# A four-layer hybrid block on one core: the weight sum of the third Strassen product made by GpSimd in SBUF instead of by an adding transfer

## The chip, the core and the metric

The kernel runs on one core of a Trainium2 chip. The metric is the device time of one execution in microseconds, median of three: 2467.82 us (2465.43 to 2470.07).

## The reference, cut to what matters

Four layers, each a mixer (RWKV-7, sliding-window attention, a spatial gating unit, gated linear attention) followed by a SwiGLU feed-forward part. Everything is float32, 512 tokens by 1024 features, 2816 hidden columns.

```python
def swiglu(x, w_in, w_out):
    gate, up = jnp.split(x @ w_in, 2, axis=-1)
    return (jax.nn.silu(gate) * up) @ w_out
...
    for i in range(DEPTH):
        hn = rmsnorm(h, norm_mix[i])
        ...
        h = h + m
        h = h + swiglu(rmsnorm(h, norm_ffn[i]), ffn_w_in[i], ffn_w_out[i])
    return rmsnorm(h, norm_final)
```

## The kernel before, in words

**The products.** Large matrix products go through `seven` (L857). It cuts the product into a 2 by 2 grid of halves and does it in seven half-size products instead of eight, with sums of weight quarters and of input quarters on the way. In the order of the code these are m1 (with weight quarter 0), m2 (quarter 1), m5 (quarters 2+0), m3 (quarter 3), m6 (2+0+3), m7 (3+2) and m4 (2+0+3+1). `load(q)` fetches a quarter into raw buffers `wraw`, issued by SP; `add(tile, q)` adds a quarter to a raw buffer that is already filled, by a transfer issued by GpSimd that accumulates while it lands. In the code `a`, `e`, `b`, `c` are the buffers of quarters 0, 1, 2, 3. So `a` and `e` are used once, `c` is added to once, and `b` three times: +0, +3, +1.

**Two pieces.** A quarter is held in two buffers ("first and second piece") of 128 partitions by 1024, 768 or 512 floats. Each piece is fetched, added to and split by itself.

**The split.** TensorE runs one-pass float32r products. So `mm` (L882) splits each raw buffer into a high part `whi` (a copy by ScalarE) and a low part `wlo` (raw minus high, by VectorE; `split`, L604) and does three matmuls for each tile. A product of width 512 is 24 matmuls of 128x512.

**Buffers.** The raw pool `wr` has 8 buffers: four quarters. `whi` and `wlo` have 4 buffers each: two quarters. PSUM has 8 banks.

**Where `seven` is called.** In each feed-forward layer (`ffn`, L809) there are six calls for the hidden columns (`hidden`, L933, weights `ffn_w_b` of width 384 and `ffn_w_a` of width 512) and three for the way back (`out_fast`, L838, weights `ffn_o_b` and `ffn_o_a`). The first two products of the next hidden block (its `a` and `e`) are done ahead of a way-back call, the other five behind it. The gating unit calls it four times, the linear attention three times in this form and twice with `rows=True`. That makes 43 calls that the change touches, with two pieces each.

**What sets the order.** No engine's order is written by hand. `Program` records every operation, then `run` (L309) places them one at a time: for each engine the ready operation with the lowest turn (its place in the code, moved by the table TURNS), if a buffer for it can be had, on a clock kept from the estimated costs in `price` (L283). A GpSimd addition is priced by `2.4` ns an element there, a transfer by 1000 ns of its engine and a shared DMA time. So an operation with another engine and cost moves others around it. On the chip each engine runs its list in order and waits by semaphores; a GpSimd transfer whose buffer isn't ready holds up all that is behind it on GpSimd, and an SP load that has no free buffer holds up all loads behind it.

All operations are recorded by one helper, so most rows of the profile have the line L253; the names of the tiles tell them apart.

Of the kernel before, what the change touches and what calls it, by code (L numbers as in the profile page):

```python
# [501 lines left out]
class K:  # L502
# [354 lines left out]
    def seven(self, w, W, x, nsub=4, rows=False):  # L857

        nc = self.nc
        m = 1024 // W
        us = [(k, min(m, nsub - k)) for k in range(0, nsub, m)] if rows else [(k, min(2, nsub - k)) for k in range(0, nsub, 2)]

        def load(q):  # L870
            t = []
            for k, n in us:
                raw = self.wr.tile([P, 1024], F32, name="wraw")[:, :n * W]
                nc.sync.dma_start(raw, w[q][:, k * W:(k + n) * W])
                t.append(raw)
            return t

        def add(a, q):
            for (k, n), t in zip(us, a):
                nc.gpsimd.dma_start(t, w[q][:, k * W:(k + n) * W], accum_op=ALU.add)  # L880

        def mm(key, ps, raw, first, last):  # L882
            xs = x(key)
            for u, (k0, n) in enumerate(us):
                hi = self.wh.tile([P, 1024], F32R, name="whi")[:, :n * W]
                lo = self.wl.tile([P, 1024], F32R, name="wlo")[:, :n * W]
                self.split(raw[u], hi, lo)
                if rows:
                    for j in range(W // P):
                        for k in range(n):  # L890
                            xh, xl = xs[(k0 + k) // 2]
                            t = slice((k0 + k) % 2 * 256, (k0 + k) % 2 * 256 + 256)
                            c = slice(k * W + j * P, k * W + (j + 1) * P)
                            self.mm3(ps[:, j * 256:(j + 1) * 256], hi[:, c], lo[:, c], xh[:, t], xl[:, t],
                                     first and k0 + k + j == 0, last and k0 + k == nsub - 1)
                    continue
                for b in range(2):
                    for k in range(n):
                        if callable(xs):
                            (xh, xl), t = xs(k0 + k), slice(b * P, (b + 1) * P)  # L900
                        else:
                            (xh, xl), t = xs[u], slice(k * 256 + b * P, k * 256 + (b + 1) * P)
                        c = slice(k * W, (k + 1) * W)
                        self.mm3(ps[b], xh[:, t], xl[:, t], hi[:, c], lo[:, c], first and k0 + k == 0, last and k0 + k == nsub - 1)
        banks = lambda: self.bank() if rows else [self.bank()[:, :W] for _ in range(2)]
        a = load(0)
        p = banks()
        mm('x11', p, a, True, True)
        yield 'm1', p
        e = load(1)  # L910
        s = banks()
        mm('x12', s, e, True, True)
        yield 'm2', s
        b = load(2)
        add(b, 0)
        r = banks()
        mm('s5', r, b, True, True)
        yield 'm5', r
        c = load(3)
        add(b, 3)  # L920
        t = banks()
        mm('s3', t, c, True, True)
        yield 'm3', t
        add(c, 2)
        mm('s6', p, b, False, True)
        yield 'm6', p
        mm('s7', p, c, False, True)
        yield 'm7', p
        add(b, 1)
        mm('x22', p, b, False, True)  # L930
        yield 'm4', p
# [1115 lines left out]
```

## Time and profile before

| | |
|---|---|
| median of three runs | 2467.82 us |
| the profiled execution, whole | 2470.02 us |
| its span on the core | 2468.3 us |
| mean granted clock | 0.997 |
| ScalarE busy | 1389.3 us (56%) |
| VectorE busy | 1930.5 us (78%) |
| GpSimd busy | 400.2 us (16%), 456 instructions |
| loads by SP (queue q1) | 226.47 MB, 27.2% of the 16 DMA engines |
| adding transfers by GpSimd (queue q0) | 171.99 MB, 39.2% of the 16 DMA engines |

The profiled execution's own time stands 1.7 us above its span, and 2.2 us above the median of the runs. Sums in the prediction are made against that execution. TensorE's two rows are matmuls (PE) and weight loads (PEld), which overlap.

### The profile page before, as it was taken

Reading aid. Unit: us, or ns where it says so; the run is one execution under the profiler, and the core shown is the slowest. Engines: PE = TensorE matmul, PEld = TensorE weight load, DVE = VectorE, ACT = ScalarE, POOL = GpSimd, SP = SyncE. Lnnn points to the kernel's source line nnn. Section 1 sums busy time; section 2 is a strip of 40 time slices with the busy share of each in tenths; the row PEclk is TensorE's granted clock in tenths of the full one; section 3 lists DMA queues with packets and bytes.
Section 4 is the critical chain, followed back from the end, with each engine's and each line's share of the span. In section 5 each row is a group of like instructions: output and inputs, shape, how many; then the busy total and the mean of one; then the engine's idle time right before and its main releaser. Section 6 shows DMA issues by size and latency. Waiting matters only on the chain.

```text
span 2468.3 us, 37524 instructions
## 1 busy us (share of the span) xinstructions
PE 2411.1 (98%) x14166; PEld 1995.9 (81%) x14166; DVE 1930.5 (78%) x3051; ACT 1389.3 (56%) x2267; POOL 400.2 (16%) x456
## 2 busy tenths in 40 slices
PE   9999999999999999999999999999999999999998
PEld 7677789987888768988887788887878788888886
DVE  8686995786779885777789886976868978886868
ACT  4545544664646476656466544854546756755555
POOL 0000000111112241121111300211111221212111
PEclk9999999999999999999999999999999999999999
DMA  5220002589898234898988835889897775989885
GB/s 170 71 71 10 11 11 81 137 226 215 208 221 187 75 107 103 192 238 192 233 189 202 218 99 153 183 201 216 200 225 182 187 181 124 187 214 227 216 211 125
DMA packets 128629, 400.85 MB, mean 162 GB/s; under 512 B 14384, under 2 KB 21040, under 8 KB 128448
## 3 DMA queue, kind: packets, MB, share of 16 engines
q0 software_dynamic: 50688, 171.99, 39.2%
q1 hardware_dynamic: 77760, 226.47, 27.2%
q8 instruction: 111, 1.82, 0.3%
q14 instruction: 70, 0.57, 0.1%
HBM read 393.95 MB, written 2.10 MB: 160 GB/s over the span
## 4 chain that ended last, share of the span: by engine, by line
PE 71%; DMA 9%; DVE 9%; ACT 5%; issue 4%; POOL 1%; SPq 0%; DVEq 0%; POOLq 0%; ACTq 0%
PE ps L253 71%; DMA wraw<-ffn_w_a 3%; DMA wraw<-ffn_w_b 2%; DVE wlo L253 2%; ACT slot L253 2%; DVE slot L253 2%; DMA wraw<-ffn_o_a 2%; ACT whi L253 1%; DVE h L253 1%; POOL wraw L253 1%; DVE et L253 1%; DMA wraw<-sg_w_v 1%; DVE mt L253 0%; DMA wraw<-gla_w_qk 0%; POOL slot L253 0%
## 5 line engine op out<-in xcount | busy, mean ns | idle before, releaser
L253 PE MATMUL ps<-whi,slot 128*128 128x512 f32 (+1 forms) x4960 | 1509.7, 385 | 13.7 <-DVE slot L253 7.4
L253 PEld LDWEIGHTS ps<-whi,slot 128*128 128x128 f32 x4960 | 923.4, 188 | 186.2 <-DVE slot L253 14.7
L253 ACT CAST whi<-wraw 128x1024 fp32r<-128x1024 f32 (+2 forms) x680 | 673.8, 997 | 619.5 <-PE ps L253 426.6
L253 DVE TENSOR_TENSOR wlo<-wraw,whi 128x1024 fp32r<-128x1024 f32 (+2 forms) x680 | 783.7, 1161 | 237.9 <-ACT whi L253 233.8
L253 PE MATMUL ps<-wlo,slot 128*128 128x512 f32 (+1 forms) x2480 | 932.7, 383 | 4.1 <-DVE wlo L253 4.1
L253 PEld LDWEIGHTS ps<-wlo,slot 128*128 128x128 f32 x2480 | 466.8, 188 | 85.7 <-DVE wlo L253 7.9
L253 PE MATMUL ps<-slot,whi 128*128 128x512 f32 (+3 forms) x976 | 276.1, 366 | 1.8 <-ACT slot L253 0.9
L253 DVE TENSOR_TENSOR slot<-ps,slot 128x512 f32<-128x512 f32 (+2 forms) x269 | 159.0, 607 | 79.7 <-PE ps L253 70.6
L253 PEld LDWEIGHTS ps<-slot,whi 128*128 128x128 f32 (+2 forms) x976 | 170.4, 184 | 40.4 <-issue 4.5
L253 POOL DMA_DIRECT2D wraw<-ffn_w_a x128 | 111.0, 879 | 483.2 <-DVE wlo L253 339.4
L253 DVE TENSOR_TENSOR h<-h,ps 128x512 f32<-128x512 f32 x240 | 159.0, 684 | 26.6 <-PE ps L253 24.3
L253 DVE TENSOR_TENSOR slot<-left,slot 128x512 fp32r<-128x512 f32 x250 | 160.2, 662 | 23.5 <-ACT slot L253 15.4
L253 PE MATMUL ps<-slot,wlo 128*128 128x512 f32 (+3 forms) x488 | 176.5, 366 | 0.0
L253 ACT CAST slot<-left 128x512 fp32r<-128x512 f32 (+1 forms) x250 | 143.4, 601 | 29.0 <-PE ps L253 18.0
L253 ACT COPY slot<-ps 128x512 f32<-128x512 f32 (+2 forms) x154 | 85.3, 566 | 72.4 <-PE ps L253 66.0
L253 PEld LDWEIGHTS ps<-slot,wlo 128*128 128x128 f32 (+2 forms) x488 | 89.5, 184 | 18.4 <-issue 3.7
L253 POOL DMA_DIRECT2D wraw<-ffn_o_a x64 | 55.9, 873 | 297.3 <-DVE wlo L253 210.5
L253 POOL DMA_DIRECT2D wraw<-ffn_w_b x64 | 55.1, 867 | 300.2 <-DVE wlo L253 99.4
L253 PE MATMUL ps<-ident,slot 128*128 128x128 f32 (+2 forms) x672 | 88.8, 265 | 6.6 <-DVE slot L253 6.4
L253 PEld LDWEIGHTS ps<-ident,slot 128*128 128x128 f32 (+2 forms) x672 | 68.8, 140 | 31.1 <-DVE slot L253 10.6
L253 DVE TENSOR_TENSOR slot<-slot 128x512 fp32r<-128x512 f32 (+7 forms) x131 | 77.2, 611 | 12.1 <-DMA slot<-slot 7.2
L253 ACT COPY left<-ps 128x512 f32<-128x512 f32 x100 | 51.0, 555 | 44.1 <-PE ps L253 44.0
(281 smaller groups left out, 2242.0 us busy)
## 6 DMA issues: line engine op xcount, KB each, us to landing
wraw<-ffn_w_a SPq DMA_DIRECT2D x128, 512.0 KB, 6.4
wraw<-ffn_w_a POOLq DMA_DIRECT2D x128, 512.0 KB, 7.9
wraw<-ffn_o_a SPq DMA_DIRECT2D x64, 512.0 KB, 5.1
wraw<-ffn_o_a POOLq DMA_DIRECT2D x64, 512.0 KB, 7.1
wraw<-ffn_w_b SPq DMA_DIRECT2D x64, 384.0 KB, 4.0
wraw<-ffn_w_b POOLq DMA_DIRECT2D x64, 384.0 KB, 6.6
wraw<-ffn_o_b SPq DMA_DIRECT2D x16, 512.0 KB, 3.9
wraw<-ffn_o_b POOLq DMA_DIRECT2D x16, 512.0 KB, 7.3
```

The lines of the kernel that those rows point to most:

```text
L253: op = self.add(eng.name, lambda: getattr(eng.target, what)(*map(real, args), **{k: real(a) for k, a in kw.items()}), *self.price(eng.name ...
```

## The change

The first of the three additions to `b` is no longer a transfer. Where `rows` isn't set, GpSimd adds `a`, which is in SBUF, to `b`, piece by piece.

```diff
         b = load(2)
-        add(b, 0)
+        if rows:
+            add(b, 0)
+        else:
+            for t, u in zip(b, a):
+                nc.gpsimd.tensor_add(t, t, u)
         r = banks()
         mm('s5', r, b, True, True)
         yield 'm5', r
```

The number of operations and their places in the code stay as they are. The additions now read `a`, so the buffers of `a` are in use until then. The order on the engines moves from the first feed-forward layer on; three places:

**GpSimd, first feed-forward layer, from the first to the second `ffn_w_a` block.** Buffers 6260 and 6283 of before are `b` of the first such block, 6614 and 6652 `b` of the second; in the change they are 6302 and 6321, and 6679 and 6708. Before:

```order
L253 DMA wraw_6260<-ffn_w_a 128x1024
L253 DMA wraw_6614<-ffn_w_a 128x1024
L253 DMA wraw_6283<-ffn_w_a 128x1024
L253 DMA wraw_6652<-ffn_w_a 128x1024
L253 DMA wraw_6614<-ffn_w_a 128x1024
L253 DMA wraw_6652<-ffn_w_a 128x1024
```

Now:

```order
L253 DMA wraw_6302<-ffn_w_a 128x1024
L253 DMA wraw_6321<-ffn_w_a 128x1024
L253 TENSOR_TENSOR wraw_6679<-wraw_6679,wraw_6533 128x1024
L253 TENSOR_TENSOR wraw_6708<-wraw_6708,wraw_6551 128x1024
L253 DMA wraw_6679<-ffn_w_a 128x1024
L253 DMA wraw_6708<-ffn_w_a 128x1024
```

The last additions of the first block stood behind and between the first additions of the second; they now stand ahead of both.

**GpSimd, first feed-forward layer, the way back `ffn_o_b` and the `ffn_w_a` block around it.** Buffers 6147 and 6170 are `b` of the way back before, 6191 and 6224 its `c`; in the change 6189 and 6216, and 6268 and 6280. Before:

```order
L253 DMA wraw_6147<-ffn_o_b 128x1024
L253 DMA wraw_6170<-ffn_o_b 128x512
L253 DMA wraw_6260<-ffn_w_a 128x1024
L253 DMA wraw_6283<-ffn_w_a 128x1024
L253 DMA wraw_6147<-ffn_o_b 128x1024
L253 DMA wraw_6170<-ffn_o_b 128x512
L253 DMA wraw_6191<-ffn_o_b 128x1024
L253 DMA wraw_6260<-ffn_w_a 128x1024
```

Now:

```order
L253 TENSOR_TENSOR wraw_6189<-wraw_6189,wraw_6053 128x1024
L253 TENSOR_TENSOR wraw_6216<-wraw_6216,wraw_6066 128x512
L253 TENSOR_TENSOR wraw_6302<-wraw_6302,wraw_5848 128x1024
L253 DMA wraw_6189<-ffn_o_b 128x1024
L253 DMA wraw_6216<-ffn_o_b 128x512
L253 TENSOR_TENSOR wraw_6321<-wraw_6321,wraw_5865 128x1024
L253 DMA wraw_6268<-ffn_o_b 128x1024
L253 DMA wraw_6302<-ffn_w_a 128x1024
```

The hidden block's sum (6302) stays ahead of the way back's second addition, and its second piece (6321) moves behind it, ahead of the addition to `c`.

**ScalarE, first feed-forward layer, from the third to the fourth `ffn_w_a` block.** Buffer 7524 is the second piece of `e` of the fourth block in both; 7559 and 7588 are its `b` before (7638 and 7670 in the change), 7234 and 7259 `c` of the third block before (7291 and 7333 in the change). Before:

```order
L253 COPY whi_7655<-wraw_7524 128x1024
L253 COPY whi_7687<-wraw_7559 128x1024
L253 COPY whi_7693<-wraw_7234 128x1024
L253 ACTIVATE slot_7615<-slot_7615,rcol_5521 128x512
L253 COPY whi_7737<-wraw_7588 128x1024
L253 COPY whi_7749<-wraw_7259 128x1024
```

Now:

```order
L253 COPY whi_7649<-wraw_7524 128x1024
L253 COPY whi_7685<-wraw_7291 128x1024
L253 COPY whi_7695<-wraw_7333 128x1024
L253 ACTIVATE slot_7610<-slot_7610,rcol_5521 128x512
L253 COPY whi_7735<-wraw_7638 128x1024
L253 COPY whi_7751<-wraw_7670 128x1024
```

The two pieces of the sum `b` stood in turn with the two pieces of the third block's `c`; both pieces of `c` are now split first.

## The prediction, made before the change was run

> **What bounds the kernel now.** The page comes first: busy shares, and the chain of work that ended last.
>
> ```profile
> PE 2411.1 (98%) x14166; PEld 1995.9 (81%) x14166; DVE 1930.5 (78%) x3051; ACT 1389.3 (56%) x2267; POOL 400.2 (16%) x456
> PE 71%; DMA 9%; DVE 9%; ACT 5%; issue 4%; POOL 1%; SPq 0%; DVEq 0%; POOLq 0%; ACTq 0%
> ```
>
> TensorE is busy for 98% of the span, so whatever the change saves elsewhere can only be had from the few gaps between matmuls. DMA stands on the chain with 9%, though; that is why the stages are read next, by the table of busy times by stretch: the part from the first feed-forward layer on, and three pieces of feed-forward layers.
>
> ```profile
> core 0: us, PE busy (x) PEld busy (x) DVE busy (x) ACT busy (x) POOL busy (x), PEclk, DMA share, GB/s
> 465.00:2468.30 2003.30, 1959.48 (x9513) 1629.32 (x9511) 1580.29 (x2300) 1162.35 (x1841) 384.89 (x422) 1.00 0.77 184
> 650.00:720.00 70.00, 69.34 (x309) 56.82 (x308) 54.10 (x66) 37.27 (x46) 14.67 (x17) 1.00 0.95 214
> 720.00:785.00 65.00, 65.00 (x307) 53.27 (x306) 57.37 (x78) 41.51 (x61) 11.41 (x15) 1.00 0.90 220
> 1200.00:1300.00 100.00, 100.00 (x463) 81.95 (x463) 79.01 (x99) 60.87 (x90) 14.99 (x19) 1.00 0.88 210
> ```
>
> The DMA engines are at 0.88 to 0.95 in these pieces, at a full clock, and yet TensorE lacks next to nothing. From 465 us on, where the changed calls are, it is idle for 2003.3 - 1959.5 = **43.8 us**. No relief of DMA or GpSimd can give more than that.
>
> **What is removed.** 86 adding transfers: one in four of those that the 43 calls issue.
>
> ```profile
> wraw<-ffn_w_a SPq DMA_DIRECT2D x128, 512.0 KB, 6.4
> wraw<-ffn_w_a POOLq DMA_DIRECT2D x128, 512.0 KB, 7.9
> wraw<-gla_w_o POOLq DMA_DIRECT2D x8, 512.0 KB, 5.8
> q0 software_dynamic: 50688, 171.99, 39.2%
> L253 POOL DMA_DIRECT2D wraw<-ffn_w_a x128 | 111.0, 879 | 483.2 <-DVE wlo L253 339.4 <-DVE slot L253 68.9 <-DMA wraw<-ffn_w_a 55.5
> ```
>
> The rows from ffn_w_a to gla_w_o, without the eight of gla_w_qk, come to 344, and a quarter of them is 86. They are about a quarter of q0's 39.2%, so some 9 to 10 points of DMA share go. What is that worth in gaps? I laid the issue and landing of every adding transfer over TensorE's gaps. The first additions run early, while their block's predecessor still computes; those whose landing the copy to the high part awaits are mostly the second and third. Of the larger gaps behind a transfer, those in which a *removed* transfer was in flight lie in seven places:
>
> ```profile
> 600.00:606.00 6.00, 2.50 (x13) 1.74 (x12) 2.93 (x3) 2.40 (x3) 0.00 (x0) 0.95 1.02 291
> 1131.00:1136.00 5.00, 3.83 (x17) 2.90 (x16) 2.75 (x5) 2.00 (x2) 0.68 (x1) 1.00 1.06 282
> 1672.00:1677.00 5.00, 4.48 (x19) 3.19 (x18) 5.00 (x8) 1.98 (x3) 1.53 (x2) 1.00 0.99 169
> 1716.00:1722.00 6.00, 4.05 (x18) 2.98 (x16) 3.54 (x4) 5.89 (x9) 0.00 (x0) 0.97 0.63 204
> 1794.00:1806.00 12.00, 9.99 (x43) 7.64 (x42) 8.46 (x10) 4.20 (x4) 0.86 (x1) 1.00 0.90 232
> 1870.00:1874.00 4.00, 3.65 (x18) 2.84 (x17) 2.42 (x3) 1.40 (x2) 0.00 (x0) 1.00 1.05 274
> 2145.00:2150.00 5.00, 4.18 (x23) 3.54 (x22) 3.12 (x5) 3.53 (x6) 2.34 (x3) 1.00 0.91 168
> ```
>
> Together they hold 43.0 - 32.7 = 10.3 us of idle TensorE. The largest shows how, in the chain of work:
>
> ```profile
> 582.86 6.33 DMA wraw<-ffn_w_a
> 589.75 0.53 POOL wraw L253
> 590.29 11.61 DMA wraw<-ffn_w_a
> 601.99 1.05 ACT whi L253
> 605.01 1.19 PE ps L253 x5
> ```
>
> A first addition waits on GpSimd for its load until 589.75; the third addition of the block ahead is queued behind it, then shares the DMA engines with it and takes 11.61 us where 7.9 is usual. The change puts the third additions ahead there. I take **-8 us** of the 10.3, between 0 and the 43.8 that bounds all of it. The GpSimd time of the removed issues (0.88 us each) hides in GpSimd's 16%.
>
> **What is added: GpSimd time, and VectorE's wait for it.** By the code's widths the 86 additions are 66 of 128x1024, 16 of 128x768 and 4 of 128x512. The nearest operation in the trace is the same in-place float32 addition at half the width: the bias rows added to `h`.
>
> ```profile
> L253 POOL TENSOR_TENSOR h<-h,slot x16: 1282/1314/2453, 783.0 to 1406.4; 128x512 f32<-128x512 f32 x16
> 783.03 3.63 POOL L253 TENSOR_TENSOR h<-h,slot 128x512 f32<-128x512 f32 x2 [2.98 <-ACT slot L253]
> 783.19 2.32 DVE L253 TENSOR_TENSOR wlo<-wraw,whi 128x1024 fp32r<-128x1024 f32 x1
> 789.99 1.21 DVE L253 TENSOR_TENSOR wlo<-wraw,whi 128x1024 fp32r<-128x1024 f32 x1
> 1405.41 2.14 DVE L253 TENSOR_TENSOR wlo<-wraw,whi 128x1024 fp32r<-128x1024 f32 x1
> ```
>
> At 1.29 us for 512 elements (undisturbed ones lie between 1.28 and 1.31) the 81,920 elements take 160 x 1.29 = 206 us of GpSimd, an estimate by plain doubling. GpSimd then stands at 400 - 76 + 206 = 530 us, far from a bound. But the rows show more: a low part that starts during such an addition takes 2.32 or 2.14 us in place of 1.21, and the second of the two additions waited for it in turn (3.63 us for the pair, not 2.6). The two exclude each other. On the page SBUF — State Buffer of the Trainium skill (section "SBUF: two separate sides") this is a rule: a VectorE operation with two SBUF inputs and a GpSimd one hold a shared port pair for a whole instruction, and the later one waits. The trace agrees with 2.32 against 1.21; without this exclusion the next term would be nothing and the sum 2467 instead of 2477. GPSIMD Engine Reference in the Trainium skill (section "Performance versus the Vector engine") speaks against plain additions on GpSimd altogether, and its 4497 ns for 2048 elements would make 180 us, an estimate by that page, and a sum one microsecond lower.
>
> The sum goes by the row's 206 us.
>
> What do VectorE's delays cost TensorE? An addition of 1024 keeps a low part waiting for up to 2.57 us. Most of that vanishes: matched one by one from 465 us on, a low part is done 5 us before its first matmul in the middle of all cases, and in a fifth of them less than 2 us before. The row of ScalarE's waits says the same; it stands idle for TensorE to free a high part, so the splits run a full set of buffers ahead. The nearest measured case is the 16 additions to `h`, 16 x 1.29 = 20.6 us. Behind them TensorE lost time twice:
>
> ```profile
> ACT whi L253 <- PE ps L253: 426.6, 270, 5.7
> 791.25 0.50 PE L253 MATMUL ps<-wlo,slot 128*128 128x512 f32 x1 [0.51 <-DVE wlo L253]
> 1410.04 1.02 PE L253 MATMUL ps<-slot,wlo 128*128 128x512 f32 x2
> 790.13 0.61 PE L253 MATMUL ps<-whi,slot 128*128 128x512 f32 x2
> ```
>
> 0.51 us at 791, and 0.4 us at 1410 (a pair takes 1.02 us where 0.61 is usual). With about 1 us for 20.6 us of additions, 206 us cost **+10 us**. The bounds: 0, since all could hide in the 5 us; and 53 us if every addition were like the two at 783 (from the pair at 790.13, two matmuls of 0.227 us, the next was due at 790.58 and came 0.67 us late, for 2.6 us of additions).
>
> **What moves: buffers and queues.** `a` must now stay until `b` is loaded and added. Before, loads follow the end of a low part to the hundredth:
>
> ```profile
> 704.60 1.22 DVE L253 TENSOR_TENSOR wlo<-wraw,whi 128x1024 fp32r<-128x1024 f32 x1
> 705.85 0.33 SPq L253 DMA_DIRECT2D wraw<-ffn_w_a  x1
> 715.96 1.23 DVE L253 TENSOR_TENSOR wlo<-wraw,whi 128x1024 fp32r<-128x1024 f32 x1 [0.40 <-ACT whi L253]
> 717.22 0.33 SPq L253 DMA_DIRECT2D wraw<-ffn_w_a  x1
> SPq L253 <- DVE wlo L253: 1247.2, 364, 17.6
> 722.81 2.01 ACT L253 CAST whi<-wraw 128x1024 fp32r<-128x1024 f32 x2 [3.45 <-PE ps L253]
> 728.96 0.40 PE L253 MATMUL ps<-whi,slot 128*128 128x512 f32 x1
> ```
>
> At 705.85 `b` of the fourth block goes into the buffer that its own `a` left at 705.82. With the change it can't; the next buffer to come free is that of `e`, at 717.19, so `b` loads **11.4 us later**. Load (6.4), addition (2.6) and half a microsecond of notice end near 726.7 for the first piece, where ScalarE split it at 722.81 and TensorE used it at 728.96. The order helps: ScalarE now splits the old block's `c` first, which gives `b` some 5 us. In 21 of the 86 pieces `b` took its own `a`'s buffer, in ten calls; I price the lateness at 0.4 us a call, **+4 us**, between 0 and 2.5 us a call (25 us).
>
> In each layer two sums of a hidden block stand on GpSimd ahead of the way back's second or third additions. What is queued behind them are transfers on which m6 and m7 wait. An addition holds them up by 2.57 us where an issue took 0.88; the adding transfers are waited for on landing, but their low parts then have the same few us of lead. I take **+3 us**, between 0 and 8 places x 2.57 = 21 us. Other order changes I can't price; they go into the range with 5 us either way.
>
> **Sum.** -8 + 10 + 4 + 3 = +9 us on 2470.0, which is 2479 against the profiled execution; the median of the runs is 2.2 us lower, so **2477 us**. A measurement of this kernel can tell about 0.2% (5 us) from no change: 2462.9 to 2472.8.
>
> **The rivals.**
> *Faster: the DMA relief reaches all gaps.* Every adding transfer that is awaited (the 9% of the chain) becomes shorter by its share of a less crowded DMA, not only the seven places. For it: 0.95 DMA share. Against it: the removed transfers run early, mostly beside loads, not beside those awaited. If half of the 43.8 us goes and the costs halve, -22 + 8 = -14 us: 2454. It needs VectorE's delays to hide.
> *No change:* the gain of 8 and the lock of 10 cancel and the buffers hide: 2468. That the change does what it says is plain from the order; that nobody feels it is this case.
> *Much slower: the lock makes VectorE the bound where it is full.* In 720:785 VectorE is busy 57.37 of 65 us; five microseconds more in a call of 38 us (24 x 7 matmuls, of which 309 went into the 70 us of 650:720, 0.227 us each) make it 102%. If half of the additions behave like the two at 783, 0.26 x 103 = 27 us come in place of 10: 2494. It decides from the point where low parts have under 2.5 us of lead; a fifth had before.
>
> **How the numbers follow.** My forecast (2473 to 2488) 0.45; much slower (2488 to 2510) 0.18; no change 0.19; faster (below 2462.9) 0.18. The range of 2460 to 2500 leaves out a good half of the faster case's lower part and the end of the slower. Chances: faster 0.18, same 0.19, slower 0.63.
>
> **What would show it.** Right: low parts of 2 to 3.7 us next to GpSimd additions of about 2.6 us; TensorE's waits for `wlo` up; VectorE's busy time up by 50 to 150 us; DMA share down by 9 points; the gap at 605 gone. Wrong: additions much longer than 2.6 us; TensorE's idle time from 465 us on below 43 us; loads of `b` behind which TensorE waits for several us (then the buffers, not the lock, are the cost).

## The result, and the profile after

The changed kernel takes **2594.57 us** (median of 4 runs, 2584.40 to 2596.75), the kernel before 2468.95 us in the same series (2465.43 to 2471.15). The ratio is **1.0501**, with a 95% interval of 1.0482 to 1.0519: slower by about 125 us, where 9 were forecast. In what follows a per cent of the time before is 24.7 us.

The page of the changed kernel first, busy times and the chain that ended last, the two lines with which the prediction began:

```profile
PE 2453.8 (95%) x14166; PEld 2015.2 (78%) x14166; DVE 2070.1 (80%) x3051; ACT 1388.4 (54%) x2267; POOL 546.5 (21%) x456
PE 63%; DVE 20%; issue 7%; ACT 5%; DMA 4%; POOL 1%; SPq 0%; DVEq 0%; POOLq 0%; ACTq 0%
```

No work was added for VectorE, and yet it is busy for 139.6 us more (2070.1 against 1930.5; an instruction counts as busy while it is held up), and its share of the chain has gone from 9% to 20%. DMA has gone from 9% to 4%. So one bound was taken away and a larger one put in its place. Next the stretch from 465 us on, in the table of busy times by stretch (PE, PEld, DVE, ACT, POOL, then granted clock, DMA share, GB/s), and the lines of the DMA view and of the groups that the forecast spoke of:

```profile
465.00:2582.70 2117.70, 2000.73 (x9508) 1647.37 (x9506) 1718.43 (x2299) 1160.37 (x1839) 529.23 (x422) 0.98 0.63 155
```

```profile
q0 software_dynamic: 38304, 130.04, 28.7%
...
wraw<-ffn_w_a SPq DMA_DIRECT2D x128, 512.0 KB, 5.1
wraw<-ffn_w_a POOLq DMA_DIRECT2D x96, 512.0 KB, 6.5
```

```profile
L253 DVE TENSOR_TENSOR wlo<-wraw,whi 128x1024 fp32r<-128x1024 f32 (+2 forms) x680 | 849.6, 1258 | 221.9 <-ACT whi L253 215.2
...
L253 POOL TENSOR_TENSOR wraw<-wraw 128x1024 f32<-128x1024 f32 (+1 forms) x86 | 221.3, 2585 | 565.3 <-DMA wraw<-ffn_w_b 111.1
```

Before, the row of the low parts is:

```profile
L253 DVE TENSOR_TENSOR wlo<-wraw,whi 128x1024 fp32r<-128x1024 f32 (+2 forms) x680 | 783.7, 1161 | 237.9 <-ACT whi L253 233.8
```

TensorE's idle time from 465 us on is 2117.7 - 2000.7 = 117.0 us, before 43.8: 73 us more. Its busy time grew too, by 41 us (2000.7 against 1959.5) at a mean granted clock of 0.98 instead of 1.00. The DMA engines did get their relief: q0 is down by 10.5 points, the loads of `ffn_w_a` land after 5.1 us instead of 6.4. The additions are about as long as forecast: 2.59 us is the mean of all three widths, and the 66 of 128x1024 take 2.34 us at the least and 2.76 in the mean, against the forecast 2.57. Low parts make 65.9 us of VectorE's 139.6; the rest is in its other operations. Which of them cost time, TensorE's own waits (us in all, times, longest) say:

```profile
PE ps L253 <- DVE slot L253: 47.6, 29, 4.6
PE ps L253 <- DVE wlo L253: 29.3, 24, 3.6
PE ps L253 <- DVE h L253: 14.8, 10, 4.4
PE ps L253 <- DVE rcol L253: 5.1, 2, 4.4
```

Before, the same view has these lines:

```profile
PE ps L253 <- DVE slot L253: 20.1, 15, 3.5
PE ps L253 <- DVE wlo L253: 4.1, 6, 1.2
PE ps L253 <- DVE h L253: 3.8, 4, 1.1
...
PE ps L253 <- DVE rcol L253: 1.0, 1, 1.0
```

These four waits for VectorE make 29.0 us before and 96.8 after, nearly all of the 73; a little over a third of the growth is behind low parts (`wlo`), the rest behind operands of other kinds: left operands and transposed tiles (`slot`), the residual (`h`), a column of factors (`rcol`). Two places show how. The first is the one that was to get better: the gap at 605 us. In the timeline (start, duration, engine, what), with an undisturbed instance of the same VectorE operation at its head:

```profile
604.59 0.75 DVE L253 SCALAR_TENSOR_TENSOR slot<-slot,ncol 128x512 f32<-128x512 f32 x1
...
607.38 5.67 POOL L253 TENSOR_TENSOR wraw<-wraw 128x1024 f32<-128x1024 f32 x2 [7.43 <-DMA wraw<-ffn_w_a]
...
608.19 2.67 DVE L253 TENSOR_TENSOR wlo<-wraw,whi 128x1024 fp32r<-128x1024 f32 x1 [1.12 <-ACT whi L253]
610.78 2.82 DVE L253 SCALAR_TENSOR_TENSOR slot<-slot,ncol 128x512 f32<-128x512 f32 x1
...
613.66 0.61 PE L253 MATMUL ps<-ident,slot 128*128 128x128 f32 x3 [4.45 <-DVE slot L253]
```

The two pieces' additions stand one behind the other on GpSimd. The low part waits for the first and takes 2.67 us in place of 1.22; the scaling behind it waits for the second and takes 2.82 in place of 0.75. TensorE stands for 4.45 us, and not for the low part, but for the scaled tile that it has to transpose. The gap at 605 has gone, and one as large has come at 609. The second place shows that the size of the VectorE operation doesn't matter:

```profile
2000.58 0.15 DVE L253 SCALAR_TENSOR_TENSOR rs_t<-ms,rs_t 128x4 f32<-128x4 f32 x1
...
2001.23 2.83 POOL L253 TENSOR_TENSOR wraw<-wraw 128x1024 f32<-128x1024 f32 x1 [3.35 <-DMA wraw<-gla_w_vg]
...
2001.79 2.30 DVE L253 SCALAR_TENSOR_TENSOR rcol<-rs_t,rcol 128x4 f32<-128x4 f32 x1
...
2004.23 1.09 PE L253 MATMUL ps<-ident,rcol 128*128 128x128 f32 x4 [4.43 <-DVE rcol L253]
```

Four elements a partition, 0.15 us for one of that form, here 2.30, until the addition ends. TensorE was idle for 4.43 us.

### The profile page after: what moved, and what is told of

It is laid out like the page before. It is cut to its first block, busy times and chain, and to the rows that moved or that the text cites. A ratio compares the mean times of both kernels' runs of the same rounds, so it can differ in the third digit from the quotient of the medians.

```text
span 2582.7 us, 37411 instructions
## 1 busy us (share of the span) xinstructions
PE 2453.8 (95%) x14166; PEld 2015.2 (78%) x14166; DVE 2070.1 (80%) x3051; ACT 1388.4 (54%) x2267; POOL 546.5 (21%) x456
## 4 chain that ended last, share of the span: by engine, by line
PE 63%; DVE 20%; issue 7%; ACT 5%; DMA 4%; POOL 1%; SPq 0%; DVEq 0%; POOLq 0%; ACTq 0%
PE ps L253 62%; DVE wlo L253 6%; DVE slot L253 6%; ACT slot L253 2%; DVE h L253 2%; DVE left L253 2%; ACT whi L253 2%; DMA wraw<-ffn_o_a 1%; DVE et L253 1%; DMA wraw<-sg_w_v 1%; POOL wraw L253 1%; DVE rs_t L253 1%; ACT left L253 0%; DMA wraw<-ffn_w_a 0%; DVE rcol L253 0%
## 5 line engine op out<-in xcount | busy, mean ns | idle before, releaser
L253 PE MATMUL ps<-whi,slot 128*128 128x512 f32 (+1 forms) x4960 | 1532.8, 389 | 30.8 <-DVE slot L253 16.2
L253 PEld LDWEIGHTS ps<-whi,slot 128*128 128x128 f32 x4960 | 935.7, 191 | 215.0 <-DVE slot L253 19.7
L253 DVE TENSOR_TENSOR wlo<-wraw,whi 128x1024 fp32r<-128x1024 f32 (+2 forms) x680 | 849.6, 1258 | 221.9 <-ACT whi L253 215.2
L253 PE MATMUL ps<-wlo,slot 128*128 128x512 f32 (+1 forms) x2480 | 945.3, 389 | 29.7 <-DVE wlo L253 29.3
L253 PEld LDWEIGHTS ps<-wlo,slot 128*128 128x128 f32 x2480 | 472.8, 191 | 120.8 <-DVE wlo L253 42.7
L253 POOL TENSOR_TENSOR wraw<-wraw 128x1024 f32<-128x1024 f32 (+1 forms) x86 | 221.3, 2585 | 565.3 <-DMA wraw<-ffn_w_b 111.1
L253 DVE TENSOR_TENSOR slot<-left,slot 128x512 fp32r<-128x512 f32 x250 | 180.5, 741 | 16.4 <-ACT slot L253 14.5
L253 POOL DMA_DIRECT2D wraw<-ffn_w_a x96 | 83.0, 865 | 338.1 <-DVE wlo L253 336.8
L253 DVE SCALAR_TENSOR_TENSOR slot<-slot,ncol 128x512 f32<-128x512 f32 (+1 forms) x96 | 76.1, 814 | 9.4 <-ACT slot L253 9.1
L253 POOL DMA_DIRECT2D wraw<-ffn_o_a x48 | 41.6, 866 | 194.6 <-DVE wlo L253 175.9
```

What stands on the lines that cost most here:

```text
L253: op = self.add(eng.name, lambda: getattr(eng.target, what)(*map(real, args), **{k: real(a) for k, a in kw.items()}), *self.price(eng.name ...
```

## The experiments

The theories: **A**, GpSimd's additions shut VectorE out; **B**, the longer hold on the first block and the moved order; **C**, what is queued behind the additions on GpSimd. All edits are at the place of the change in `seven`. "In the changed order" means that the planner was still told of a GpSimd addition, and another instruction was issued in its place. The edits are cut to the lines that matter. e3, e4, e8, e13 and e14 add 8 columns of the first block and leave the rest of it out of the sum, e7 leaves it out altogether, so only their times are of use. All ratios are against the kernel before on the same chip.

| kernel | median us | ratio, 95% interval |
|---|---|---|
| e7 before's order, no first transfer, no sum | 2453.9 | 0.9935 (0.9916 to 0.9954) |
| e3 changed order, 8 columns summed | 2456.3 | 0.9955 (0.9942 to 0.9968) |
| e6 before, first block held | 2469.4 | 1.0001 (0.9989 to 1.0014) |
| e1 changed order, adding transfers | 2499.0 | 1.0129 (1.0106 to 1.0153) |
| e8 as e3, GpSimd filling an unused tile | 2505.8 | 1.0139 (1.0107 to 1.0172) |
| e4 as e3, GpSimd filling the first block's buffer | 2509.6 | 1.0169 (1.0144 to 1.0194) |
| e2 changed, additions in quarters | 2559.3 | 1.0363 (1.0329 to 1.0396) |
| e13 as e3, full addition into the first block's buffer | 2577.9 | 1.0446 (1.0418 to 1.0474) |
| e15 GpSimd additions in e6's order | 2586.8 | 1.0480 (1.0447 to 1.0512) |
| the change | 2594.6 | 1.0501 (1.0482 to 1.0519) |

**e3: the addition's length taken away.**

```diff
-                nc.gpsimd.tensor_add(t, t, u)
+                op = nc.gpsimd.tensor_add(t, t, u)
+                op.call = lambda t=t[:, :8], u=u[:, :8]: nc.gpsimd.target.tensor_add(t.real(), t.real(), u.real())
```

> The changed kernel, with only the first 8 columns of each piece added on GpSimd; the rest of the first block is left out of the sum. Order, buffers, waits and the relief of the DMA engines stay as in the changed kernel, only the addition's length goes. Theory A (the additions' length, by VectorE): 2455 to 2475 us, and against the kernel with the adding transfers in this order it shows what the relief of the DMA engines is worth (-8 us by the prediction). Theory B (late loads and order): 2560 us or more. Theory C (GpSimd's queue): as A.

2456.25 us, 0.45% faster than before. With the same order, buffers and waits the whole loss is gone, and 5.46 points with it (135 us). So B is out, and it is the addition's length that costs.

**e1: the adding transfer back, in the changed order.**

```diff
+                op = nc.gpsimd.tensor_add(t, t, u)
+                op.call = lambda t=t, v=w[0][:, k * W:(k + n) * W]: nc.gpsimd.target.dma_start(t.real(), v, accum_op=ALU.add)
```

> The changed kernel's order of instructions and its buffers, with the first block still held until the sum is made; only the sum itself is made by the adding transfer again, at the addition's place in GpSimd's row. So everything of the change is here but the addition and the relief of the DMA engines. Theory A (GpSimd's addition shuts VectorE out for 2.6 us at a time, and that is the cost): 2465 to 2485 us. Theory B (the later load of the block that is summed, and the moved order, are the cost): 2560 us or more. Theory C (what is queued behind the long additions on GpSimd is the cost): as A, since an issue takes 0.88 us here.

2499.02 us, between what A and B expected, and so by itself no decision. Together with e3 it says that the transfers cost 1.74 points in this order. That is more than e7 gives below: the order was made for a sum of 2.7 us, and a transfer takes 7. So the 30 us that e1 loses against the kernel before are not in the change: e3 has the same order and none of this loss.

**e7 and e6: what the removed transfers were worth, and what the hold costs, in before's kernel.**

```diff
+            op = nc.gpsimd.dma_start(t, w[0][:, k * W:(k + n) * W], accum_op=ALU.add)
+            if not rows:
+                op.call = lambda t=t[:, :8]: nc.gpsimd.target.tensor_add(t.real(), t.real(), t.real())
```

> The kernel before in its own order and buffers, without the first adding transfer of the 43 calls; at its place GpSimd works on 8 columns. The first block is left out of the sum. What the removed transfers are worth by themselves: -8 us by the prediction, so 2455 to 2465 us; -43 us if it is worth here what it was worth in the changed order (2499.0 against 2456.3), so about 2426 us.

2453.93 us, -0.65% (-0.84 to -0.46), or -16 us: between the two expectations, twice the prediction's -8. It isn't only in the seven places that a transfer became shorter: loads of `ffn_w_a` take 5.2 us in the middle of all, before 6.4.

```diff
+                op = nc.gpsimd.dma_start(t, v, accum_op=ALU.add, hold=u)
+                op.call = lambda t=t, v=v: nc.gpsimd.target.dma_start(t.real(), v, accum_op=ALU.add)
```

> The kernel before, adding transfers and all, with the one difference that the planner holds the first block's buffer until the adding transfer is issued; the order that follows is the planner's. Holding the buffer (loads that come 11 us later) as the cause of the 30 us by which the changed order with transfers was slower: 2485 to 2505 us. If the changed order was at fault and not the holding: within 10 us of the kernel before.

2469.40 us: nothing, within 0.14%. The later loads of `b` cost nothing that can be measured. From e7 to e3, which puts the hold and the changed order on top of the removed transfers, it is 0.20 points (5 us), which the two intervals do not tell from nothing.

**e4 and e8: GpSimd busy for as long, but reading nothing.** e4 fills the first block's buffer behind the 8 columns, e8 a tile that nobody uses:

```diff
+                    nc.gpsimd.target.tensor_add(t[:, :8].real(), t[:, :8].real(), u[:, :8].real())
+                    for _ in range(3):
+                        nc.gpsimd.target.memset(u.real(), 0.0)
```

```diff
+                    for _ in range(22 * t.shape[-1] // 1024):
+                        nc.gpsimd.target.memset(self.scrap.real(), 0.0)
```

> The same with 8 columns added, and behind them three fills with zero of the first block's buffer (128x1024 each), by then unused: some 2.8 us of GpSimd's time, worked out from 0.31 us for a fill of 256 columns, in which it writes and reads nothing. The first block is left out of the sum but for 8 columns. Theory A (VectorE is shut out while GpSimd reads two operands): as the kernel with 8 columns, within 10 us. Theory C (GpSimd's time and what is queued behind it is the cost): 2560 us or more. If VectorE is shut out by any operation of GpSimd, low parts of over 2 us appear here too.

> The changed kernel with 8 columns added, and behind them GpSimd fills a tile of 64 columns that nobody uses, 22 times (16 or 11 for the narrower pieces): some 2.8 us by 0.2 us for 128 columns and 0.31 for 256. The first block is left out of the sum but for 8 columns. Against the kernel with the fills of the first block's buffer (2509.6 us) the buffer comes free at once here; only GpSimd's row is taken. GpSimd's queue as the cost of the 53 us: 2495 to 2520 us. The late release of the first block's buffer as the cost: 2455 to 2470 us.

2509.58 and 2505.82 us: 2.14 and 1.84 points over e3 (53 and 45 us). The fills take GpSimd 232 us in e4 and 274 in e8, where the additions of the change take it 221. A had expected e4 within 10 us of e3, and this is wrong: GpSimd's time by itself costs something, as C says, though not the whole. e8, in which the buffer comes free at once, costs as much as e4, so it is the queue and not the buffer. The waits of ScalarE for adding transfers and loads of the four feed-forward weights show it, in e8 and then in e3:

```profile
ACT whi L253 <- DMA wraw<-ffn_w_a: 34.8, 15, 6.3
...
ACT whi L253 <- DMA wraw<-ffn_o_a: 32.6, 17, 5.1
...
ACT whi L253 <- DMA wraw<-ffn_o_b: 30.3, 12, 4.9
ACT whi L253 <- DMA wraw<-ffn_w_b: 30.1, 16, 4.6
```

```profile
ACT whi L253 <- DMA wraw<-ffn_w_a: 24.4, 12, 3.8
...
ACT whi L253 <- DMA wraw<-ffn_o_a: 18.8, 14, 3.1
...
ACT whi L253 <- DMA wraw<-ffn_w_b: 12.8, 10, 2.6
...
ACT whi L253 <- DMA wraw<-ffn_o_b: 3.0, 1, 3.0
```

That is 127.8 us in e8 and 59.0 in e3. (In the kernel before, where the first additions are still among the transfers, the four make 98.2.)

Followed buffer by buffer, the 264 later adding transfers from 465 us on are issued 0.40 us after their low part in e3, 0.92 in e4 and 1.19 in e8, where 49 of them come more than 2 us late. What did *not* come in e4 are long low parts. Their row by tile has count, shortest, median and longest in ns:

```profile
L253 DVE TENSOR_TENSOR wlo<-wraw,whi x680: 288/1219/2322, 13.5 to 2489.2; 128x1024 fp32r<-128x1024 f32 x131, 128x768 fp32r<-128x768 f32 x28, 128x512 fp32r<-128x512 f32 x11
```

Before, the same row begins with 285/1220/2323, so it is the same but for 1 to 3 ns. The 66 low parts of 1024 beside a fill from 465 us on take 1.22 us in the mean and 1.23 at the most. Fills don't shut out VectorE's work on two operands. Two scalings of 128x4 with one operand (`ncol`) did end with the fill beside them, after 0.36 and 0.44 us in place of 0.16.

**e13: the same place, but with reads.** Instead of the three fills one addition, its result put into the first block's buffer, so that the split of the sum does not wait for it:

```diff
+                    nc.gpsimd.target.tensor_add(t[:, :8].real(), t[:, :8].real(), u[:, :8].real())
+                    nc.gpsimd.target.tensor_add(u.real(), t.real(), u.real())
```

> The changed kernel, with 8 columns added, and behind them a full addition whose result goes to the first block's buffer, by then unused, instead of the three fills. The first block is left out of the sum but for 8 columns. Places, buffers and dependencies are those of the kernel with the fills (2509.6 us); the one difference is that GpSimd reads two operands for 2.4 to 2.8 us where it only wrote for 2.9. Exclusion by reads: 2580 to 2610 us, and low parts of over 2 us as in the changed kernel. If the 85 us came from the sum being ready later: 2500 to 2520 us.

2577.86 us: 2.77 points (68 us) above e4, though it occupies GpSimd for less time: 2.51 us for 128x1024, where the three fills take 3 x 0.96 = 2.88. The groups of e13 and then of e4, and the low parts' row by tile of e13:

```profile
L923 POOL TENSOR_TENSOR wraw<-wraw 128x1024 f32<-128x1024 f32 x66 | 165.8, 2513 | 8.6 <-POOL wraw L922 2.3 <-issue 1.3
```

```profile
L924 POOL MEMSET wraw<- 128x1024 f32 x198 | 190.2, 960 | 14.0 <-issue 1.3 <-POOL wraw L922 1.1
```

```profile
L253 DVE TENSOR_TENSOR wlo<-wraw,whi x680: 285/1219/3418, 14.1 to 2556.3; 128x1024 fp32r<-128x1024 f32 x131, 128x768 fp32r<-128x768 f32 x28, 128x512 fp32r<-128x512 f32 x11
```

The longest low part of e13 is 3.42 us, as in the changed kernel (4.04) and unlike e4 (2.32, as before). An example, in e13's timeline:

```profile
683.76 2.40 POOL L923 TENSOR_TENSOR wraw<-wraw 128x1024 f32<-128x1024 f32 x1
684.09 3.16 DVE L253 TENSOR_TENSOR wlo<-wraw,whi 128x1024 fp32r<-128x1024 f32 x1
```

All 34 low parts of 1024 that begin within an addition of e13 end 1.08 or 1.09 us after it, wherever in it they begin; in the changed kernel 36 of 37 do. So they get next to nothing of their 1.22 us done before the addition is over. The two kernels differ in what GpSimd reads, so A is shown: reads of two operands shut VectorE out. In SBUF — State Buffer of the Trainium skill, section "SBUF: two separate sides", a VectorE operation with two SBUF inputs contends only with a GpSimd operation that reads SBUF. The pair e4 and e13 agrees: 1.23 us at the most beside fills, 3.42 beside reads. What is left to the changed kernel is 0.55 points (14 us), with intervals that all but touch. There the split waits for the full sum, some 2.4 us longer than for the 8 columns in e13; that this makes the 14 us was not tested.

**e14: reads of one operand.**

```diff
+                    for _ in range(3):
+                        nc.gpsimd.target.tensor_scalar(u.real(), u.real(), 0.5, None, op0=ALU.mult)
```

> The same with three scalings by 0.5 of the first block's unused buffer in place of the full addition: GpSimd reads one operand and writes. The first block is left out of the sum but for 8 columns. How long they take no run has shown. If any read of GpSimd shuts VectorE's two-operand work out, low parts of over 1.9 us appear beside them and the time is over 2530 us; if only two-operand reads do, low parts stay at 1.22 us and the time near 2510 us for scalings of about 1 us each.

2923.15 us, a ratio of 1.1846 (1.1814 to 1.1877). The time tells nothing on the question, since one scaling takes 2.97 us in the mean (2.77 undisturbed) instead of about 1, and three hold GpSimd's queue for 9:

```profile
L924 POOL TENSOR_SCALAR wraw<-wraw 128x1024 f32<-128x1024 f32 x198 | 587.9, 2969 | 19.0 <-POOL wraw L922 1.4 <-issue 1.3
...
L253 DVE TENSOR_TENSOR wlo<-wraw,whi 128x1024 fp32r<-128x1024 f32 (+2 forms) x680 | 796.4, 1179 | 649.3 <-ACT whi L253 555.9 <-POOL wraw L924 91.3
```

The low parts do tell something: of 115 of 128x1024 beside a scaling 22 take over 1.4 us and the longest 2.06.

```profile
1237.21 6.30 POOL L924 TENSOR_SCALAR wraw<-wraw 128x1024 f32<-128x1024 f32 x2
1237.64 2.06 DVE L253 TENSOR_TENSOR wlo<-wraw,whi 128x1024 fp32r<-128x1024 f32 x1
```

So a read of one operand holds VectorE up as well, but for 0.84 us at the most and not for the 2.8 of the instruction. All 31 low parts that took over 1.25 us end 0.65 or 0.66 us before the end of the scaling beside them. In an undisturbed scaling of 2.77 us that lets VectorE begin after 0.9 us; low parts that began later than that were not held. By the page's rule in the same section of the Trainium skill the loser would wait for the whole instruction; for two operands that agrees with the rows here, for one it does not.

**e2: the addition in quarters.** `c` is a quarter of the columns.

```diff
+                    for j in range(0, 4 * c, c):
+                        nc.gpsimd.target.tensor_add(t[:, j:j + c].real(), t[:, j:j + c].real(), u[:, j:j + c].real())
```

> The changed kernel, with each addition given to GpSimd as four additions of a quarter of the columns, one after the other. Theory A (VectorE is shut out by whole additions): a VectorE operation waits for at most one quarter, some 0.65 us, before its own turn, so 2480 to 2550 us, and low parts of more than 2.5 us all but gone. Theory B (late loads and order): about 2595, no change against the changed kernel. Theory C (GpSimd's queue): 2595 or above, since four pieces take GpSimd as long as one or longer.

2559.31 us: 1.38 points better than the change, and 9 us above the upper end that A gave. Low parts beside an addition are shorter (1.58 us in the mean instead of 2.45, 6 over 2 us instead of 37), but now each quarter waits for VectorE in its turn:

```profile
L923 POOL TENSOR_TENSOR wraw<-wraw 128x256 f32<-128x256 f32 x264 | 294.0, 1195 | 350.2 <-DMA wraw<-ffn_o_a 67.2 <-DMA wraw<-ffn_w_a 60.7 <-DVE left L253 51.2
```

A quarter takes 1.20 us in the mean and 0.72 at the least where 0.65 was expected. Finer pieces move the waiting from VectorE to GpSimd's queue.

**e15: the addition in another order.** Against e6:

```diff
-                op.call = lambda t=t, v=v: nc.gpsimd.target.dma_start(t.real(), v, accum_op=ALU.add)
+                op.call = lambda t=t, u=u: nc.gpsimd.target.tensor_add(t.real(), t.real(), u.real())
```

> GpSimd's additions in the order that the planner made for the kernel with the adding transfers and the first block held (2469.4 us with the transfers): the planner thinks of the sum as a transfer and counts on it later. Exclusion as the cause, whatever the order: 2560 to 2610 us. If the order made for a short addition is a main part of the loss: 2540 us or less.

2586.83 us, against 2469.40 with transfers in the same order. The loss goes with the addition, not with the order. This is also the cleanest pair for the whole effect: the same list for every engine, transfer against addition, +4.79 points.

**e5 and e9 to e12: halves of the change, and VectorE instead of GpSimd.** e9 has the change in the 24 calls of hidden blocks alone, e10 in the other 19; e5 makes the sum on VectorE in all calls, e11 and e12 in the same two halves. The edit of e11, against the change (`hid` is set by the call in `hidden` alone):

```diff
-        if rows:
+        if rows or not hid:
             add(b, 0)
         else:
             for t, u in zip(b, a):
-                nc.gpsimd.tensor_add(t, t, u)
+                nc.vector.tensor_add(t, t, u)
```

> The change in the 24 calls of the hidden blocks alone (48 of the 86 additions, 55% of their time on GpSimd: 32 x 2.76 + 16 x 2.07 = 121 of 221 us); the other 19 calls keep the adding transfer. If the loss goes with the time of the additions: 0.55 x 125 = 69 us, 2538 us. If it is made where VectorE has operations without a lead (the left operands of the calls around it), the two halves differ by over 20 us from these shares.

> The other half: the change in the 19 calls that are not hidden blocks (38 additions, 34 x 2.76 + 4 x 1.73 = 101 us of GpSimd), the hidden blocks keep the adding transfer. By the time of the additions: 0.45 x 125 = 56 us, 2525 us; and both halves together make up the 125 us of the whole change, within 20 us, if they don't act on each other.

> The sum is made on VectorE instead of GpSimd, and the planner is told so, so it sets its own order. 86 additions of about 1.2 us (as a low part of the same size) are some 95 us more for VectorE, nothing is shut out, nothing is queued on GpSimd, and the relief of the DMA engines stays. If the exclusion and GpSimd's queue are the loss of the change (85 and 53 us by the runs so far): 2445 to 2490 us. If the loss is that VectorE has no room for anything more: 2520 us or above.

> The sum on VectorE in the 24 calls of the hidden blocks alone, the adding transfer in the other 19. By its share of the 26 us that VectorE's sums cost in all calls: 2483 us. If it beats the kernel before, 2464 us or less.

> The sum on VectorE in the 19 calls that are not hidden blocks, the adding transfer in the 24 hidden blocks. By its share of the 26 us: 2482 us. VectorE has less to do between two hidden blocks' ends than within them (no gate, no product of gate and up), so it may be had for nothing here, and then the relief of 38 transfers shows: 2460 to 2465 us.

| sum made by | hidden blocks | the others | all 43 calls |
|---|---|---|---|
| GpSimd | e9: 2530.31, 1.0250 (1.0211 to 1.0289) | e10: 2546.18, 1.0309 (1.0265 to 1.0352) | 2594.57, 1.0501 |
| VectorE | e11: 2477.35, 1.0050 (1.0033 to 1.0068) | e12: 2482.72, 1.0063 (1.0044 to 1.0081) | e5: 2496.12, 1.0101 (1.0080 to 1.0123) |

GpSimd's halves make 5.59 points together, the whole 5.01: nearly additive. The hidden blocks come to 2.50 points, a little under their share of 2.76; the others to 3.09, some 21 us over theirs, which is 2.0 us for an addition against 1.3. Why those cost more no run tells. The sum on VectorE costs 97 us of its time:

```profile
L253 DVE TENSOR_TENSOR wraw<-wraw 128x1024 f32<-128x1024 f32 (+1 forms) x86 | 97.0, 1144 | 10.8 <-DMA wraw<-ffn_w_a 7.8 <-DMA wraw<-ffn_o_a 1.4 <-DMA wraw<-sg_w_o 0.7
```

The kernel loses 1.01% by it, 6 us more than the upper end expected, and neither half beats the kernel before. VectorE has no room that is free, but 97 us of plain work on it cost far less than the 139.6 us that the change made it stand. No version found here beats the kernel before: by e7, removing these transfers is worth 16 us in before's order, and each place tried for the sum costs more.

## Why the prediction was wrong

The sign was right, and the mechanisms named are the ones that came; the sum was wrong by its second term above all and by its fourth, and the range did not hold the time. Along one row of runs the 5.01 points are -0.65 for the removed transfers (e7), +0.20 for hold and order (e3), +2.14 for GpSimd's time (e4), +2.77 for its reads (e13) and +0.55 for the rest.

- **-8 us for the removed transfers.** -16 us (-21 to -11) by e7. Right in kind, half of the size: loads became shorter beyond the seven places that I had counted.
- **+10 us for VectorE's wait.** This is the step that failed: "Most of that vanishes: matched one by one from 465 us on, a low part is done 5 us before its first matmul". Reads alone make +68 us (e13 against e4), more than the upper bound of 53. Three things were wrong in it. The lead was measured for low parts only (and matched again by the planner's order it is 4.3 us in the middle, 3.5 for the blocks that are added to, not 5), but VectorE works in order, and the operations with no lead (`slot`, `h`, `rcol`) are shut out or stand behind one that is: TensorE's waits for these grew from 24.9 to 67.5 us, those for `wlo` from 4.1 to 29.3. The two pieces' additions come one behind the other, so that VectorE loses twice within 6 us, as at 607, and a lead of 5 us is used up. And the scale of 1 us for 20.6 us of additions came from one kind of place, the bias rows of `h`; here it was 68 for 221, six times as much. (The 221 hold GpSimd's own waits for VectorE: at 2.34 to 2.41 us for an undisturbed addition of 1024 the 81,920 elements would be some 190, an estimate, and not the 206 of the doubled row.)
- **+4 us for the later loads.** Nothing for the hold (e6), 5 us with the order (e3 against e7), within the noise. Right.
- **+3 us for GpSimd's queue, at most 21.** This term failed too. Where GpSimd is busy for as long or somewhat longer and low parts are not shut out, it costs 45 to 53 us (e8, e4). In the changed kernel this doesn't show as a queue: adding transfers follow their low part after 0.49 us, before after 0.42. There the low part itself ends late, and the addition with it. So the 135 us from e3 to the change can't be divided cleanly between queue and exclusion: 53 and 68 is the division along this row of experiments, with 14 left over.
- **Order, 5 us either way.** e15 and the change differ by 0.21 points, 5 us, within their intervals. Right.
- **The rival "much slower".** The lock is what happened, with a price far too low: half of the additions at 0.26 us for each us, 27 us in all. But it doesn't take a full VectorE: with the gap at 2093 it was busy for 15.7 of 25 us.

What was to show it came: additions of 2.6 us, low parts of 2 to 4 us beside them, VectorE's busy time up by 139.6 us, q0 down by 10.5 points, TensorE's waits for `wlo` up. The gap at 605 went and came back at 609. The first two signs for "wrong" that I had named did not come: the additions were not much longer than 2.6 us, and TensorE's idle time rose. It was the effect of the additions that was not as forecast.

A part of the loss isn't idle time. Cut into pieces of 25 us from 475 us to just before the end, 18 have a granted clock under 0.985 after the change, 3 before; 25 us times what is missing to 1, summed, makes 39 us after and 5 before. They lie where the gaps are. Three of them:

```profile
1625.00:1650.00 25.00, 20.71 (x102) 19.88 (x101) 24.79 (x40) 13.30 (x25) 10.03 (x7) 0.83 0.51 141
2000.00:2025.00 25.00, 20.77 (x113) 18.28 (x114) 20.95 (x31) 17.22 (x25) 5.44 (x4) 0.86 0.46 115
2075.00:2100.00 25.00, 18.79 (x109) 15.94 (x108) 15.67 (x15) 7.12 (x9) 6.78 (x4) 0.86 0.67 180
```

So some 34 us of the 114 by which the span grew go with a lower clock around gaps: single ones of 3 to 5 us (those that end at 2004 and 2093 among them), or several smaller ones close together, as at 1642 and 1646. At such places the granted clock is one half for 3.4 to 10.2 us at a time (0.50 from 2003.2 to 2010.0). That the gaps cause it was not tested; it goes with them in the other runs too: 2 us missing in e3, 9 in e4, 33 in e13. The prediction had no term for it.

## What to carry to other kernels

Before an elementwise operation is moved to GpSimd, count what VectorE does in the same time with all its operands in SBUF, however small: beside an addition it waited for the addition's end, and so did all that was behind it. That isn't a matter of two operands alone: all five VectorE operations with one operand that met an addition were held to its end as well (one of 128x4, `lrs`, took 2.27 us in place of 0.17). Measure the lead of every kind of VectorE result that TensorE waits for, not only of the one that is most frequent, and count two additions in a row as two such waits. A busy share of 20% on an in-order engine is no cover for what is queued behind a long instruction on it.

## What the runs showed of the hardware

- GpSimd's fills did not delay VectorE's two-operand work (66 low parts of 1.22 us took 1.23 at the most). Its two-operand additions did until their end, wherever the low part began (up to 4.04 us), its one-operand scalings only for their first 0.9 us (by up to 0.84 us).
- A float32 scaling in place of 128x1024 takes GpSimd 2.77 us undisturbed, longer than an addition with two operands (2.34 to 2.41); a fill of the same size takes 0.96. An addition of 8 columns takes 0.19 us undisturbed.
- VectorE's two-operand operations with one operand in PSUM were not held up: the residual's additions (`h`, 128x512) took 0.68 us in the mean before, after the change and in e2, e5, e8 and e15, and the 17 of them that met an addition of the change 0.69 at the most.
- The eight gaps of 3 to 5 us in TensorE's work after the change went with a granted clock of 0.86 to 0.93 in the 25 us around them.
